# Attention inside a PE-bound network: scores of two heads issued in turn in the two row halves, softmaxes interleaved, near biases loaded when the job opens

## The chip, the cores and the metric

The kernel runs on one core of a Trainium2 chip. The core has a matmul engine (TensorE, PE in the profile; its weight loads are listed as PEld), a vector engine (VectorE, DVE), an activation engine (ScalarE, ACT), a general engine (GpSimd, POOL) and an engine that issues the DMA transfers (SyncE, SP). Each works through its own instruction list in order, and they wait for each other through semaphores. The metric is device time in microseconds, as the median of several runs.

## The reference, cut to what matters

Two layers of a transformer-like network work on 256 context and 256 latent tokens of 1024 channels. Each layer is a gated feed-forward half, a token mixer with four branches, and a second feed-forward half. Two branches of the mixer are attention with four heads of 64 channels, and latent queries see the local latent keys and all context keys:

```python
def neighbourhood_attention(q, k, v, kc, vc, rel_bias):
...
    s_loc = jnp.einsum('brnqhd,brnkchd->brnhqkc', qg, kg).astype(jnp.float32) * scale + bias
    s_loc = jnp.where(col_valid[None, None, :, None, :, None, :], s_loc, NEG_INF)
    s_ctx = jnp.einsum('brnqhd,blhd->brnhql', qg, kc).astype(jnp.float32) * scale
...
    probs = jax.nn.softmax(scores, axis=-1).astype(v.dtype)
```

The window branch does the same with a mask in place of the bias and with one more score, a learned sink per head, in the softmax. Context queries see the 256 context keys alone; they are needed only in the first layer, because the output is the latent stream.

## The kernel before, in words

All activations lie channels on partitions, tokens along the free side. The large products are made to fp32 accuracy from two fp32r parts: every weight tile is loaded by SP (line 128, three buffers `w`), split by ACT (`wh`, line 150) and DVE (`wl`, line 151), and each product of 128 channels is three PE instructions (`mm3`, lines 191 to 193). PE accumulates in eight banks: `A` has three, `B` two, `C`, `D` and `E` one each. One ordered list fixes the sequence of weight tiles.

Smaller work is placed beside the large products. A generator (`job`) does a piece and yields the nanoseconds of product time after which it wants to go on. `term` calls `spend(1.25 * columns)` after its three products (640 for 512 columns, 320 for 256), which advances a planning clock and lets at most one waiting piece run. `until(key)` runs waiting pieces at once until a job is done. This order is the program's; the build's scheduler then orders the instructions of each engine, and lets an instruction go ahead of earlier ones when those still wait for a buffer or an operand and it does not.

The mixer opens two attention jobs with the generator `attend`: "near" right after the keys, queries and values of the neighbourhood branch, and "window" later, within the gated merge. A unit is two heads and 128 queries. There are eight units per job in layer 0 (four context, four latent) and four in layer 1 (latent only). `attend` overlaps three units per round: `turn` transposes the weights of unit b through bank `C` (line 658) and ACT copies them out (line 660); `scores` multiplies keys and queries of unit a into a bank `B` and calls `softmax`; `values` multiplies the turned weights of unit c into bank `D` (line 689). An fp32 matmul of the program shows as two PE instructions in the profile. In `scores` (line 675) a head uses partitions 0 to 63 or 64 to 127, 256 keys at a time; latent units have two such halves of keys, context units one. In `values` the two heads already alternate, one into columns 0 to 63 of the array and one into 64 to 127.

`softmax` serves one head: bias and row maximum on DVE (lines 636 to 644), Exp with its sum on ACT (line 646), reciprocal and scaling on DVE (lines 650 and 651).

`na_bias` loads the bias of two heads with eight small DMAs into two tiles of tag `a` (line 567) and adds the mask into two tiles of tag `nb` (line 571). It is called from `scores`, when the first head of a pair has issued its products. Tag `a` has four buffers and also serves the softmax weights and their transposes. Tag `nb` has two and also serves a running sum of the norms.

Of the kernel before, what the change touches and what calls it, by code (L numbers as in the profile page):

```python
# [10 lines left out]
AF = mybir.ActivationFunctionType  # L11
ALU = mybir.AluOpType
# [10 lines left out]
NEG = -1e30  # L23
# [12 lines left out]
class Net:  # L36
# [15 lines left out]

    BUFS = dict(b=12, nb=2, ya=4, yp=4, m=8, a=4, l=5, r=3, t=2)
    BANKS = dict(A=3, B=2, C=1, D=1, E=1)
# [12 lines left out]

# [1 line left out]
    def plan(self):  # L69
# [85 lines left out]
    def apart(self, k):  # L155
        """Weights kept beside the ring: the last ones of a phase, whose two segments lie far apart."""
        return k[0] == "wo" and k[2] == 3 or k[0] == "dn" and k[3:] == (1, 7)
# [7 lines left out]

# [1 line left out]
    def later(self, ns, fn):  # L167
# [19 lines left out]

# [1 line left out]
    def mm3(self, ps, wh, wl, xh, xl, first, last):  # L189
# [110 lines left out]

# [1 line left out]
    def norm(self, l, i, rng):  # L302
# [93 lines left out]
    def first_tiles(self, W, P, H):  # L396
        """The first hidden tiles, as far as the modulation of their operands has come."""
        def terms(m, j):
            for k in (2 * j, 2 * j + 1):
                for g in range(2):  # L400
                    self.term(P[m][g], W[m], 1024 * g, H, *ALL, k)

        self.first_step(0)
        for j in range(4):
            terms(0, j)
            if j < 3:
                self.first_step(j + 1)
            terms(1, j)

    def finish_stream(self, parts, last, add, nxt):  # L410
        """Last output chunks by segment, each segment's norm beside the products that follow."""
        for r in parts:
            for c in last:
                add(c, r)
                for s in self.segs(r):
                    if nxt:
                        self.norm_square(nxt, c, s)
# [84 lines left out]

# [1 line left out]
    def softplus_terms(self, l):  # L504
# [52 lines left out]
    def na_bias(self, l, pr):  # L557
        nc = self.nc
        src = self.a["nb"]
        nb = []  # L560
        for h in (2 * pr, 2 * pr + 1):
            raw = self.blk("a", (128, 2, 4, 64))
            for qb in range(2):
                for r in range(2):
                    o = src.offset + (l * 4 + h) * 465 + (7 - (2 * qb + r)) * 31 - 48
                    ap = bass.AP(tensor=src.tensor, offset=o, ap=[[1, 64], [31, 4], [1, 64]])
                    nc.sync.dma_start(raw[64 * r:64 * r + 64, qb], ap)  # L567
            t = self.blk("nb", (128, 2, 4, 64))
            mask = self.cst[:, C_NM:C_NM + 256].rearrange("p (a b) -> p a b", b=64)
            for qb in range(2):  # L570
                nc.vector.tensor_tensor(t[:, qb], raw[:, qb, :, ::-1], mask, op=ALU.add)
            nb.append(t[:].rearrange("p q a b -> p q (a b)"))
        return nb
# [57 lines left out]

    def softmax(self, S, nk, bias, sink):
        nc = self.nc
        m = self.small((128, 4), "mx", 6)
        if bias is not None:
            nc.vector.tensor_tensor_reduce(out=S[:, 256:512], in0=S[:, 256:512], in1=bias, scale=1.0, scalar=NEG,
                                           op0=ALU.add, op1=ALU.max, accum_out=m[:, 0:1])
            nc.vector.tensor_reduce(m[:, 1:2], S[:, 0:256], axis=AX, op=ALU.max)
            nc.vector.tensor_tensor(m[:, 0:1], m[:, 0:1], m[:, 1:2], op=ALU.max)
        else:  # L640
            nc.vector.tensor_reduce(m[:, 0:1], S[:, 0:nk], axis=AX, op=ALU.max)
        if sink is not None:
            nc.vector.tensor_tensor(m[:, 0:1], m[:, 0:1], sink, op=ALU.max)
        nc.vector.tensor_scalar(m[:, 0:1], m[:, 0:1], -1.0, None, op0=ALU.mult)
        p = self.blk("a")
        nc.scalar.activation(p[:, :nk], S[:, :nk], AF.Exp, bias=m[:, 0:1], accum_out=m[:, 1:2])
        if sink is not None:
            nc.scalar.activation(m[:, 2:3], sink, AF.Exp, bias=m[:, 0:1])
            nc.vector.tensor_tensor(m[:, 1:2], m[:, 1:2], m[:, 2:3], op=ALU.add)
        nc.vector.reciprocal(m[:, 3:4], m[:, 1:2])  # L650
        nc.vector.tensor_scalar(p[:, :nk], p[:, :nk], m[:, 3:4], None, op0=ALU.mult)
        return p

# [9 lines left out]
    def attend(self, step, segs, out, keys, queries, value, biases, sink):  # L663
        """One unit is two heads and 128 queries; scores, turned weights and values of three units overlap."""
        nc = self.nc
# [3 lines left out]

        def scores(u, hh):  # L670
            pr, sg, qb = u
            rows, qw = slice(64 * hh, 64 * hh + 64), slice(128 * qb, 128 * qb + 128)
            S = self.ps("B")
            for j in range(nk(u) // 256):
                nc.tensor.matmul(S[:, 256 * j:256 * j + 256], queries(sg, j)[rows, pr, qw], keys(j, pr)[rows],  # L675
                                 start=True, stop=True)
            if pr not in bias:
                bias[pr] = biases(pr)
            P[u, hh] = self.softmax(S, nk(u), bias[pr](hh, qb) if sg else None, sink(pr, hh))

        def values(u):
# [9 lines left out]
            if qb == 1:  # L691
                if len(out) == pr:
                    out.append(self.blk("ya"))
                nc.scalar.activation(out[pr][:, 256 * sg:256 * sg + 256], y, AF.Copy)

        while self.pending:
            yield 300
        for i in range(len(U) + 2):
            a, b, c = (U[i - d] if 0 <= i - d < len(U) else None for d in range(3))
            if b:  # L700
                T[b, 0] = self.turn(P.pop((b, 0)), nk(b))
                yield step
            if a:
                scores(a, 0)
                yield step
            if c:
                values(c)
                yield step
            if b:
                T[b, 1] = self.turn(P.pop((b, 1)), nk(b))  # L710
                yield step
            if a:
                scores(a, 1)
            yield 2 * step
# [43 lines left out]
    def mixer(self, l, H, nxt):  # L758
# [19 lines left out]

        # the first products take the operands chunk by chunk, as the norm delivers them
        two = lambda: self.blk("b", (128, 2, 256))  # L780
# [37 lines left out]

        # short convolution
        view = lambda q: q[:, lo:hi].rearrange("p (s t) -> p s t", s=ns)  # L820
# [43 lines left out]

        # gated merge
        M, MP = [None] * KC, [None] * KC
# [170 lines left out]
```

## Time and profile before

| what | value |
|---|---|
| median of 3 runs | 2096.6 us (2094.93 to 2097.59) |
| span of the profiled execution | 2092.9 us |
| median less that span | 3.7 us |
| PE, PEld | 2065.0, 1755.2 us busy |
| DVE, ACT, POOL | 1325.4, 808.5, 86.1 us busy |
| mean granted clock of PE | 0.995 of 2.4 GHz |
| attention, layer 0: near, window | about 464 to 568, 637 to 730 us |
| attention, layer 1: near, window | about 1663 to 1725, 1772 to 1826 us |

The span runs from the first to the last instruction of one profiled execution; what lies around it is in the runs' times alone. A matmul's busy time holds its fill and drain, which overlap with its neighbours, so start times of consecutive matmuls tell more of cost than durations do. "Idle before" is the time an engine stood still in front of an instruction, with what ended it behind the arrow.

### The profile page before, as it was taken

The numbers are of one execution on the slowest core, as the hardware profiler recorded it, in microseconds if no ns is written. First come the engines' busy times: TensorE is split into PE (matmuls) and PEld (weight loads), VectorE is DVE, ScalarE is ACT, GpSimd is POOL, SyncE is SP. The second block draws the span as 40 slices with busy tenths as digits, with TensorE's granted clock in tenths as the row PEclk, the third lists the DMA queues.
The fourth block names the chain that finished last, engine by engine and source line by source line (L and its number), as shares of the span: only waits on it lengthen the run. The fifth ranks groups of instructions, "written<-read, shape, count | busy, mean of one in ns | idle before, by whom it ended". The sixth has DMA issues, their size and how long they took to land.

```text
span 2092.9 us, 29695 instructions
## 1 busy us (share of the span) xinstructions
PE 2065.0 (99%) x11937; PEld 1755.2 (84%) x11937; DVE 1325.4 (63%) x2393; ACT 808.5 (39%) x1321; POOL 86.1 (4%) x90
## 2 busy tenths in 40 slices
PE   7999999999999999999999999999999999999999
PEld 4888888896797788888888888788888989999999
DVE  4887887476546545677533367778844768775554
ACT  3322222365434434332222233222223656564443
POOL 0000000110010000100000010000001101000000
PEclk9999999999999999999999999999999999999999
DMA  9454555412122124145432234445543234363453
GB/s 331 181 182 173 202 199 164 137 69 52 63 91 76 63 100 145 70 161 182 154 116 88 75 130 161 162 170 201 194 117 133 74 87 141 128 226 143 171 196 118
DMA packets 61403, 294.46 MB, mean 141 GB/s; under 512 B 14672, under 2 KB 16336, under 8 KB 38224
## 3 DMA queue, kind: packets, MB, share of 16 engines
q1 hardware_dynamic: 61264, 292.55, 39.9%
q8 instruction: 94, 1.54, 0.3%
q14 instruction: 45, 0.37, 0.1%
HBM read 291.48 MB, written 1.05 MB: 140 GB/s over the span
## 4 chain that ended last, share of the span: by engine, by line
PE 94%; DMA 2%; issue 2%; SPq 0%; DVE 0%; POOL 0%; ACT 0%; POOLq 0%; DVEq 0%; ACTq 0%
PE A L191 19%; PE A L192 18%; PE A L193 18%; PE B L191 11%; PE B L193 11%; PE B L192 11%; PE B L675 2%; PE D L689 1%; DMA b<-in_mod 1%; PE D L265 1%; PE C L658 1%; DMA a<-in_nb 1%; PE E L728 1%; SPq L567 0%; PE E L601 0%
## 5 line engine op out<-in xcount | busy, mean ns | idle before, releaser
L150 ACT ACTIVATE wh<-w 128x1024 fp32r<-128x1024 f32 (+2 forms) x476 | 430.4, 906 | 870.9 <-PE A L192 403.9
L151 DVE TENSOR_TENSOR wl<-w,wh 128x1024 fp32r<-128x1024 f32 (+2 forms) x476 | 490.3, 1031 | 316.6 <-ACT wh L150 311.8
L191 PE MATMUL A<-h,wh 128*128 128x512 f32 (+1 forms) x1440 | 511.4, 355 | 6.2 <-ACT wh L150 3.8
L193 PE MATMUL A<-h,wl 128*128 128x512 f32 (+1 forms) x1440 | 497.6, 346 | 0.0
L192 PE MATMUL A<-h,wh 128*128 128x512 f32 (+1 forms) x1440 | 497.0, 345 | 0.0
L191 PEld LDWEIGHTS A<-h,wh 128*128 128x128 f32 x1440 | 273.8, 190 | 64.7 <-issue 18.6
L256 DVE SCALAR_TENSOR_TENSOR ya<-w,sc,ya 128x512 f32<-128x512 f32 x448 | 310.2, 747 | 13.3 <-DMA w<-in_mod 12.1
L193 PEld LDWEIGHTS A<-h,wl 128*128 128x128 f32 x1440 | 273.8, 190 | 34.2 <-DVE wl L151 1.7
L192 PEld LDWEIGHTS A<-h,wh 128*128 128x128 f32 x1440 | 274.0, 190 | 30.3 <-issue 1.1
L191 PE MATMUL B<-h,wh 128*128 128x512 f32 (+1 forms) x736 | 262.0, 356 | 0.0
L192 PE MATMUL B<-h,wh 128*128 128x512 f32 (+1 forms) x736 | 261.7, 356 | 0.0
L193 PE MATMUL B<-h,wl 128*128 128x512 f32 (+1 forms) x736 | 261.6, 355 | 0.0
L191 PEld LDWEIGHTS B<-h,wh 128*128 128x128 f32 x736 | 140.0, 190 | 19.9 <-ACT wh L150 0.4
L192 PEld LDWEIGHTS B<-h,wh 128*128 128x128 f32 x736 | 139.7, 190 | 19.6 <-issue 0.4
L193 PEld LDWEIGHTS B<-h,wl 128*128 128x128 f32 x736 | 139.7, 190 | 19.4
L455 DVE TENSOR_TENSOR t<-t,B 128x512 f32<-128x512 f32 (+1 forms) x88 | 54.2, 619 | 118.7 <-PE B L193 117.6
L330 POOL TENSOR_TENSOR nb<-nb,l 128x256 f32<-128x256 f32 x45 | 45.9, 1037 | 1351.9 <-ACT l L328 1351.9
L191 PE MATMUL A<-b,wh 128*128 128x512 f32 (+1 forms) x246 | 85.1, 346 | 0.0
L193 PE MATMUL A<-b,wl 128*128 128x512 f32 (+1 forms) x246 | 85.0, 345 | 0.0
L192 PE MATMUL A<-b,wh 128*128 128x512 f32 (+1 forms) x246 | 84.9, 345 | 0.0
L191 PE MATMUL B<-b,wh 128*128 128x512 f32 (+1 forms) x204 | 73.5, 360 | 0.0
L192 PE MATMUL B<-b,wh 128*128 128x512 f32 (+1 forms) x204 | 73.4, 360 | 0.0
(271 smaller groups left out, 2996.1 us busy)
## 6 DMA issues: line engine op xcount, KB each, us to landing
w<-in_gu SPq DMA_DIRECT2D x88, 1024.0 KB, 4.8
w<-in_mod SPq DMA_DIRECT2D x64, 1024.0 KB, 4.8
w<-in_dn SPq DMA_DIRECT2D x64, 704.0 KB, 4.0
w<-in_gb SPq DMA_DIRECT2D x64, 640.0 KB, 3.9
w<-in_fm SPq DMA_DIRECT2D x10, 1024.0 KB, 4.8
w<-in_tm SPq DMA_DIRECT2D x10, 1024.0 KB, 4.9
w<-in_wo SPq DMA_DIRECT2D x8, 1024.0 KB, 4.8
b<-in_mod SPq DMA_DIRECT2D x20, 256.0 KB, 5.7
```

The lines of the kernel that those rows point to most:

```text
L150: nc.scalar.activation(hi[i][:, :e], t[:, o:o + e], AF.Copy)
L151: nc.vector.tensor_tensor(lo[i][:, :e], t[:, o:o + e], hi[i][:, :e].bitcast(F32), op=ALU.subtract)
L191: mm(ps, wh, xh, start=first, stop=False)
L192: mm(ps, wh, xl, start=False, stop=False)
L193: mm(ps, wl, xh, start=False, stop=last)
L256: nc.vector.scalar_tensor_tensor(acc, w[:, k], sv, acc, op0=ALU.mult, op1=ALU.add)
L265: nc.tensor.matmul(g[32 * q:32 * q + 32, :], self.sel[:, j], self.part[s - 1 + q // 2][q % 2], start=(r in (1, 5)), stop=last, tile_positi ...
L330: nc.gpsimd.tensor_tensor(n["acc"][s], n["acc"][s], sq, op=ALU.add)
L455: nc.vector.tensor_tensor(s[:, lo:hi], s[:, lo:hi], ps[1][:, lo:hi], op=ALU.mult)
L658: nc.tensor.transpose(pt[:, j], p[:, 128 * j:128 * j + 128], self.ident)
L675: nc.tensor.matmul(S[:, 256 * j:256 * j + 256], queries(sg, j)[rows, pr, qw], keys(j, pr)[rows], start=True, stop=True)
L689: nc.tensor.matmul(y[64 * hh:64 * hh + 64, 128 * qb:128 * qb + 128], value(j, pr, hh), T[u, hh][:, j], start=(j == 0), stop=(j == n - 1), ...
```

## The change

`scores` takes both heads of a unit at once. For each half of the keys it issues head 0's product (rows 0 to 63) and then head 1's (rows 64 to 127), each into its own bank `B`. `softmax` works on both heads: maximum, bias and Exp of head 0, then of head 1, then one addition of the sinks and one reciprocal for both, then the two scalings. In a round of `attend` the order becomes `values` of c, `turn` of b's head 0, `scores` of a, `turn` of b's head 1, with steps of 1, 1, 2 and 2 where there were five pieces with steps of 1, 1, 1, 1 and 2.

The biases of both head pairs are requested when the job opens, before it waits for its operands. Their raw tiles have a tag of their own, `nr`, with four buffers, `nb` has four instead of two, and `a` six instead of four. The scratch that the build sets aside in SBUF for DMAs shrinks to 1024 bytes a partition. Some comments go as well and are left out of the diff.

```diff
@@ -50,7 +50,7 @@
         self.n += 1
         return f"{s}{self.n}"
 
-    BUFS = dict(b=12, nb=2, ya=4, yp=4, m=8, a=4, l=5, r=3, t=2)
+    BUFS = dict(b=12, nb=4, nr=4, ya=4, yp=4, m=8, a=6, l=5, r=3, t=2)
     BANKS = dict(A=3, B=2, C=1, D=1, E=1)
 
     def blk(self, tag, shape=(128, 512), dt=F32):
...
@@ -559,7 +559,7 @@
         src = self.a["nb"]
         nb = []
         for h in (2 * pr, 2 * pr + 1):
-            raw = self.blk("a", (128, 2, 4, 64))
+            raw = self.blk("nr", (128, 2, 4, 64))
             for qb in range(2):
                 for r in range(2):
                     o = src.offset + (l * 4 + h) * 465 + (7 - (2 * qb + r)) * 31 - 48
...
@@ -630,26 +630,32 @@
         self.later(3000, scale)
 
     def softmax(self, S, nk, bias, sink):
-        nc = self.nc
-        m = self.small((128, 4), "mx", 6)
-        if bias is not None:
-            nc.vector.tensor_tensor_reduce(out=S[:, 256:512], in0=S[:, 256:512], in1=bias, scale=1.0, scalar=NEG,
-                                           op0=ALU.add, op1=ALU.max, accum_out=m[:, 0:1])
-            nc.vector.tensor_reduce(m[:, 1:2], S[:, 0:256], axis=AX, op=ALU.max)
-            nc.vector.tensor_tensor(m[:, 0:1], m[:, 0:1], m[:, 1:2], op=ALU.max)
-        else:
-            nc.vector.tensor_reduce(m[:, 0:1], S[:, 0:nk], axis=AX, op=ALU.max)
-        if sink is not None:
-            nc.vector.tensor_tensor(m[:, 0:1], m[:, 0:1], sink, op=ALU.max)
-        nc.vector.tensor_scalar(m[:, 0:1], m[:, 0:1], -1.0, None, op0=ALU.mult)
-        p = self.blk("a")
-        nc.scalar.activation(p[:, :nk], S[:, :nk], AF.Exp, bias=m[:, 0:1], accum_out=m[:, 1:2])
-        if sink is not None:
-            nc.scalar.activation(m[:, 2:3], sink, AF.Exp, bias=m[:, 0:1])
-            nc.vector.tensor_tensor(m[:, 1:2], m[:, 1:2], m[:, 2:3], op=ALU.add)
-        nc.vector.reciprocal(m[:, 3:4], m[:, 1:2])
-        nc.vector.tensor_scalar(p[:, :nk], p[:, :nk], m[:, 3:4], None, op0=ALU.mult)
-        return p
+        nc = self.nc
+        m = self.small((128, 2, 4), "mx", 6)
+        P = []
+        for hh in range(2):
+            v = m[:, hh]
+            if bias is not None:
+                nc.vector.tensor_tensor_reduce(out=S[hh][:, 256:512], in0=S[hh][:, 256:512], in1=bias(hh), scale=1.0,
+                                               scalar=NEG, op0=ALU.add, op1=ALU.max, accum_out=v[:, 0:1])
+                nc.vector.tensor_reduce(v[:, 1:2], S[hh][:, 0:256], axis=AX, op=ALU.max)
+                nc.vector.tensor_tensor(v[:, 0:1], v[:, 0:1], v[:, 1:2], op=ALU.max)
+            else:
+                nc.vector.tensor_reduce(v[:, 0:1], S[hh][:, 0:nk], axis=AX, op=ALU.max)
+            if sink(hh) is not None:
+                nc.vector.tensor_tensor(v[:, 0:1], v[:, 0:1], sink(hh), op=ALU.max)
+            nc.vector.tensor_scalar(v[:, 0:1], v[:, 0:1], -1.0, None, op0=ALU.mult)
+            P.append(self.blk("a"))
+            nc.scalar.activation(P[hh][:, :nk], S[hh][:, :nk], AF.Exp, bias=v[:, 0:1], accum_out=v[:, 1:2])
+            if sink(hh) is not None:
+                nc.scalar.activation(v[:, 2:3], sink(hh), AF.Exp, bias=v[:, 0:1])
+        if sink(0) is not None:
+            nc.vector.tensor_tensor(m[:, :, 1:2], m[:, :, 1:2], m[:, :, 2:3], op=ALU.add)
+        nc.vector.reciprocal(m[:, :, 3:4], m[:, :, 1:2])
+        for hh in range(2):
+            nc.vector.tensor_scalar(P[hh][:, :nk], P[hh][:, :nk], m[:, hh, 3:4], None, op0=ALU.mult)
+        return P
 
     def turn(self, p, nk):
         nc = self.nc
...
@@ -661,22 +667,23 @@
         return pT
 
     def attend(self, step, segs, out, keys, queries, value, biases, sink):
         nc = self.nc
         U = [(pr, sg, qb) for pr in range(2) for sg in segs for qb in range(2)]
         P, T, Y, bias = {}, {}, {}, {}
         nk = lambda u: 512 if u[1] else 256
 
-        def scores(u, hh):
+        def scores(u):
             pr, sg, qb = u
-            rows, qw = slice(64 * hh, 64 * hh + 64), slice(128 * qb, 128 * qb + 128)
-            S = self.ps("B")
+            qw = slice(128 * qb, 128 * qb + 128)
+            S = [self.ps("B"), self.ps("B")]
             for j in range(nk(u) // 256):
-                nc.tensor.matmul(S[:, 256 * j:256 * j + 256], queries(sg, j)[rows, pr, qw], keys(j, pr)[rows],
-                                 start=True, stop=True)
-            if pr not in bias:
-                bias[pr] = biases(pr)
-            P[u, hh] = self.softmax(S, nk(u), bias[pr](hh, qb) if sg else None, sink(pr, hh))
+                for hh in range(2):
+                    rows = slice(64 * hh, 64 * hh + 64)
+                    nc.tensor.matmul(S[hh][:, 256 * j:256 * j + 256], queries(sg, j)[rows, pr, qw], keys(j, pr)[rows],
+                                     start=True, stop=True)
+            P[u] = self.softmax(S, nk(u), (lambda hh: bias[pr](hh, qb)) if sg else None, lambda hh: sink(pr, hh))
 
         def values(u):
             pr, sg, qb = u
...
@@ -693,24 +700,23 @@
                     out.append(self.blk("ya"))
                 nc.scalar.activation(out[pr][:, 256 * sg:256 * sg + 256], y, AF.Copy)
 
+        for pr in range(2):
+            bias[pr] = biases(pr)
         while self.pending:
             yield 300
         for i in range(len(U) + 2):
             a, b, c = (U[i - d] if 0 <= i - d < len(U) else None for d in range(3))
-            if b:
-                T[b, 0] = self.turn(P.pop((b, 0)), nk(b))
-                yield step
-            if a:
-                scores(a, 0)
-                yield step
             if c:
                 values(c)
                 yield step
             if b:
-                T[b, 1] = self.turn(P.pop((b, 1)), nk(b))
+                T[b, 0] = self.turn(P[b][0], nk(b))
                 yield step
             if a:
-                scores(a, 1)
+                scores(a)
+                yield 2 * step
+            if b:
+                T[b, 1] = self.turn(P.pop(b)[1], nk(b))
             yield 2 * step
 
     def recurrence(self, segs, out, U, bd, sp2, hb, step):
...
@@ -1023,7 +1029,7 @@
     from concourse.bass_utils import run_bass_kernel_spmd
 
     A = layout(**{k: np.asarray(v) for k, v in inputs.items()})
-    nc = bacc.Bacc("TRN2", target_bir_lowering=False, num_devices=1)
+    nc = bacc.Bacc("TRN2", target_bir_lowering=False, num_devices=1, dynamic_dma_scratch_size=1024)
     arrays, a = {}, {}
     for k, v in A.items():
         arrays[f"in_{k}"] = v
```

## Rows read from the trace of the kernel before

**Rows 1.** Spans and granted clock; the page's busy time by engine.

```profile
core 0: 2092.9 us, clock 0.995
...
PE 2065.0 (99%) x11937; PEld 1755.2 (84%) x11937; DVE 1325.4 (63%) x2393; ACT 808.5 (39%) x1321; POOL 86.1 (4%) x90
```

**Rows 2.** The page's chain that ended last, by line.

```profile
PE A L191 19%; PE A L192 18%; PE A L193 18%; PE B L191 11%; PE B L193 11%; PE B L192 11%; PE B L675 2%; PE D L689 1%; DMA b<-in_mod 1%; PE D L265 1%; PE C L658 1%; DMA a<-in_nb 1%; PE E L728 1%; SPq L567 0%; PE E L601 0%
```

**Rows 3.** Windows, first near attention: length, busy PE, PEld, DVE, ACT, POOL, clock, DMA.

```profile
464.00:568.00 104.00, 100.87 (x495) 73.18 (x494) 65.28 (x158) 54.77 (x99) 0.00 (x0) 0.98 0.21 55
```

**Rows 4.** Waits of PE: total us, times, longest us.

```profile
PE C L658 <- DVE a L651: 4.6, 2, 3.1
...
PE B L675 <- ACT a L646: 1.5, 1, 1.5
```

**Rows 5.** Timeline of PE around a latent and a context score call: start, us.

```profile
478.90 0.40 PE L192 MATMUL A<-h,wh 128*128 128x512 f32 x1
479.13 0.40 PE L193 MATMUL A<-h,wl 128*128 128x512 f32 x1
479.46 1.13 PE L675 MATMUL B<-b,b 64*128 64x256 f32 x4
...
480.85 0.40 PE L192 MATMUL A<-h,wh 128*128 128x512 f32 x1
...
513.99 0.40 PE L193 MATMUL A<-h,wl 128*128 128x512 f32 x1
514.31 0.70 PE L675 MATMUL B<-b,b 64*128 64x256 f32 x2
...
515.27 0.39 PE L192 MATMUL A<-h,wh 128*128 128x512 f32 x1
```

**Rows 6.** Lines by form, ACT's Exp: count, busy us, mean ns, idle before.

```profile
L646 ACT ACTIVATE a<-B,mx 128x512 f32<-128x512 f32 x32 | 21.9, 685 | 25.4 <-DVE mx L644 20.8 <-PE D L689 4.4
...
L646 ACT ACTIVATE a<-B,mx 128x256 f32<-128x256 f32 x16 | 7.6, 472 | 14.7 <-DVE mx L644 10.5 <-PE D L689 3.9 <-PE C L658 0.2
```

**Rows 7.** Timeline of the value products in layer 1's near attention.

```profile
1686.12 1.09 PE L689 MATMUL D<-a,b 128*64 128x128 f32 x16
...
1697.29 0.43 PE L689 MATMUL D<-a,b 128*64 128x128 f32 x2
```

**Rows 8.** Timeline of the bias loads of head pair 1, layer 0.

```profile
510.99 6.63 SPq L567 DMA_DIRECT2D a<-in_nb  x8
...
517.66 0.42 DVE L571 TENSOR_TENSOR nb<-a,cst 128x256 f32<-128x256 f32 x1 [3.46 <-DMA a<-in_nb]
...
521.31 0.41 PE L658 MATMUL C<-cst,a 128*128 128x128 f32 x2 [3.13 <-DVE a L651]
```

**Rows 9.** Windows behind the two stalls (columns as in rows 3).

```profile
523.30:526.80 3.50, 3.50 (x21) 2.54 (x19) 3.50 (x10) 0.38 (x1) 0.00 (x0) 0.51 0.51 180
1700.90:1707.80 6.90, 5.43 (x29) 4.09 (x28) 4.36 (x18) 2.86 (x7) 0.00 (x0) 0.51 0.10 42
```

**Rows 10.** Timeline of SP early in the run.

```profile
40.21 0.33 SPq L767 DMA_DIRECT2D bd<-in_bd  x1
58.87 0.33 SPq L128 DMA_DIRECT2D w<-in_mod  x1
```

**Rows 11.** Lines by form, softmax and transposes (columns as in rows 6).

```profile
L660 ACT ACTIVATE a<-C 128x512 f32<-128x512 f32 x32 | 18.9, 592 | 10.8 <-PE C L658 7.7 <-DVE nb L571 3.1
L651 DVE TENSOR_SCALAR a<-a,mx 128x512 f32<-128x512 f32 x32 | 15.5, 484 | 1.3
L638 DVE TENSOR_REDUCE mx<-B 128x1 f32<-128x256 f32 x32 | 13.5, 422 | 0.7
...
L646 ACT ACTIVATION_READ_ACCUMULATOR a<-B,mx 128x1 f32 x48 | 9.3, 194 | 0.0
L650 DVE RECIPROCAL mx<-mx 128x1 f32<-128x1 f32 x48 | 7.7, 160 | 7.1 <-ACT a L646 6.5
...
L646 ACT ACT_TABLE_LOAD x5 | 6.4, 1283 | 0.1
```

## Prediction

> **What bounds the kernel now.** I read the busy shares first: the matmul engine PE is busy 99% of the span [rows 1]. Busy matmul time alone does not prove a bound, so next came the chain of work that ended last: the large products of lines 191 to 193 hold 88% of the span, the score products of line 675 hold 2% and the loads of `in_nb` 1% [rows 2]. Everything PE does is on the path; whatever PE no longer has to do, or no longer waits for, comes off the end one for one as long as the other engines keep up. In the stretch of the first near attention the vector engine DVE is busy 65.3 of 104 us and the scalar engine ACT 54.8 [rows 3], so there is room to run some 10% faster there. The third view is PE's own waits: within the attention jobs they are two waits for `a` of line 651 (the scaled softmax, 4.6 us) and one for `a` of line 646 (1.5 us) [rows 4]. The rest of the 28 us without PE work (2092.9 - 2065.0) stands elsewhere, and the change does not touch it.
>
> **Scores side by side.** A head's score product contracts over 64 channels and so uses half the rows of the array. It runs between full products, and what it costs is what it pushes them apart. Latent queries (two key halves, four PE instructions, as an fp32 product is two): from the product in front at 479.13 to the second one behind at 480.85 are 1.72 us; undisturbed products stand 0.23 apart, so 1.72 - 0.46 = 1.26 us. Context queries (two instructions): 515.27 - 513.99 - 0.46 = 0.82 us [rows 5]. The Exp counts give the calls: 32 with 512 keys, 16 with 256 [rows 6]. All scores: 32 x 1.26 + 16 x 0.82 = 53.4 us of PE's path. Inside a call, two more instructions add 1.13 - 0.70 = 0.43 us, so 0.215 each; of the 1.26 us, 0.86 is streaming and 0.40 is the cost of getting in and out of the half-array shape (0.82 - 0.43 = 0.39 says the same).
>
> The change issues both heads' products in turn, one into rows 0 to 63 and one into rows 64 to 127, each into a bank of its own. No row of before shows two row halves at once, so I bound it. Nothing at all, if the second bank is not free in time and the pair falls apart into two calls as now; a loss I exclude, as no instruction is added. If the pair stays together but runs one after the other, 24 entries and exits are saved, 24 x 0.40 = 9.5 us. Best: they run together, a pair costs what one call does now, and half of 53.4 goes: 26.7 us. The nearest row is line 689, where the two heads' value products lie in two column halves and are written in turn. One head's first two instructions alone took 0.43 us; all 16 took 1.09 [rows 7]. So the other 14 took 0.66; at 0.108 each (half of 0.215, half the columns) they would take 1.51 in series, and 0.65 if two always run in lockstep. That is lockstep to within the reading. I take the best end, 26.7 us.
>
> One rule speaks against that. The Trainium skill, TensorE: Matmul & The Clock Gate, section "Part 3: Packing small matmuls — row/col tiling", says that matmuls start and end strictly in program order; with two instructions per fp32 product, the second of head 0 then keeps head 1 back by one place. By that rule a pair has one place more, 0.215 us x 24 = 5.2 us, and the sum would be 21.5 instead of 26.7. The trace disagrees for column halves, where the reading was 0.65 predicted by lockstep against 0.66 taken.
>
> **Bias loads.** The second stall belongs to the near bias. Today the biases of head pair 1 are loaded only when its first scores are issued: eight loads leave SP from 510.99 in 6.63 us, DVE's bias addition at 517.66 stood 3.46 us waiting for the load, and with DVE in order the softmax scaling behind it came late, so that PE idled 3.13 us at line 658 [rows 8]. In the second layer the same thing costs the other two waits, 1.47 + 1.54 us [rows 4]. After these idle times the granted clock is 0.51, its lower level of 1.2 GHz, for 3.5 and 6.9 us, with PE busy 3.50 and 5.43 us of them [rows 9]; work at half clock loses half its time: 1.75 + 2.7 us. The stall is worth 3.13 + 1.47 + 1.54 + 1.75 + 2.7 = 10.6 us.
>
> After, all 16 loads of a layer are issued when the job opens, into four tiles of their own (`nr`) and not into the shared ring `a`, and there are four `nb` tiles instead of two, so pair 1 no longer waits for pair 0. The build lets a load out as soon as its buffer is free: `bd`, asked for by the mixer, left at 40.21 [rows 10]. So I expect layer 0's loads far ahead of the 464 us where the attention begins, and layer 1's once layer 0's additions are done. What it costs: SP time and traffic. Sixteen loads at 6.63 / 8 = 0.83 us are 13.3 us of SP; if they go out behind `bd` they fit before the next weight load at 58.87, 18.7 us later [rows 10]. Without that cover they push a weight load back by 13.3 us in each layer, so the bounds are 0 and 26.6 us; I take 1 us, since among PE's waits in the attention jobs none is for a weight [rows 4]. The eight bias additions per layer stay eight and sit in DVE's slack [rows 3]. The bounds of the gain are 0 (the DVE wait just moves to another place) and 10.6; I take 10.6, because the loads lose the two buffer waits that made them late. What could be late next is the softmax itself.
>
> **Interleaved softmaxes and the new order.** Per pair of heads one reciprocal is saved and, with a sink, one addition: 24 x 0.16 = 3.8 us of DVE [rows 11], off the path, worth 0. But head 0's weights now wait for head 1's Exp. With reductions of 0.42 (two per head), some three small operations of 0.16, Exp 0.685 plus 0.194 for its sum and scaling 0.484 [rows 6, 11], the chain from scores to scaled weights is about 1.3 + 0.88 + 0.16 + 0.48 = 2.8 us today and 2.6 + 0.88 + 0.16 + 0.48 = 4.1 after. From the scores to `turn` of head 0 the new order leaves two double steps and a single one: in layer 0, 870 and 1740 ns of planned time round up to 2 and 3 groups of three products (3 x 0.23 = 0.69 us, the plan's 640 ns), so 8 x 0.69 = 5.5 us plus the value products. That holds 4.1 with 1.4 to spare; worth 0.
>
> Tighter: `values` now comes first in the round, a double step behind `turn` of head 1: 3 x 0.69 = 2.1 us where it was 9 x 0.69 = 6.2. The transposes (4 x 0.108) and the copy out (0.592) need 1.0 us [rows 11], so 1.1 is left for ACT's queue. Bounds: 0, and the last rival below. I take 0: the rows show DVE and ACT a third or more idle there [rows 3], and two more `a` buffers take away the wait for a free one. The smaller DMA scratch only makes room for the new tiles.
>
> **Sum.** 26.7 + 10.6 - 1 = 36.3 us off the profiled 2092.9 gives a span of 2056.6. The median of the runs, 2096.6, lies 3.7 above the span, so 2060 us, 1.7% faster. This kernel's runs agree to 0.13%, so 0.2% is about what a measurement can tell from no change.
>
> **Rivals.**
> Row halves do not overlap: 9.5 instead of 26.7, and 2060 becomes 2077. For it: no row shows row halves at once. Against: column halves run in lockstep. Chance 14%.
> The pair overlaps, but head 1's first pass waits for head 0's second: one place more per pair, 24 x 0.215 = 5.2 us, 2065. Against: the 14 instructions of [rows 7] would then need seven places of 0.108, 0.76 us, and took 0.66. The skill's rule above is this case. Chance 8%.
> The bias stall moves instead of going: DVE waits for an early load, or a weight load is late behind 16 bias loads. 5 to 12 us back: 2065 to 2072. For it: the stalled addition came 6.7 us after the first issue [rows 8], and each layer now sends twice as many loads at once. Against: four own buffers. Chance 12%.
> The other side: `values` waits for `turn`. If ACT has a table load (1.283) and both heads' Exps with their sums (0.88 each) ahead of the copy, that is 3.0 us against 1.1 of slack, 1.9 late per unit; 24 units make 46 us, and 2060 becomes 2106. It decides from 36.3 / 24 = 1.5 us late per unit on. Against: the tables change five times in the whole run at line 646 [rows 11], so it cannot strike each unit. Chance 4%.
> My forecast, 2055 to 2064: 62%.
>
> Range: 2054 (the forecast's low end, with a little for a stall I did not see) to 2078, which takes in the strict order, the moved stall and the serial case and leaves out about 1 in 10; the serial case sets the upper end. Faster 0.94, same 0.02, slower 0.04.
>
> **What would show it.** Line 675: 160 matmuls still, but in 24 groups; 8 instructions of a latent pair in about 1.15 us if they overlap, 2.0 if not. Waits of PE at lines 658 and 675 gone, the clock at its upper level through both near attentions, the `in_nb` loads of layer 0 far ahead of 464 us. No new wait of PE at line 689 for the `a` that ACT copies out. Wrong would be: pairs of 2.0 us, or PE idle over 1 us per unit in front of the values.

## The result, and the profile after

The changed kernel takes 2064.15 us (median of 4, 2062.49 to 2066.55), before beside it 2095.76: a ratio of 0.9848, 95% interval 0.9836 to 0.9860. That is 31.6 us faster, where 36.6 were forecast (2060). The profiled executions differ by less, 2092.9 - 2064.8 = 28.1 us, because that of before was one of its quicker ones and that of after its slowest of four.

The page of after, answering to [rows 1] and [rows 2]: span, busy times, the chain by line.

```profile
core 0: 2064.8 us, clock 0.995
...
PE 2037.9 (99%) x11937; PEld 1740.5 (84%) x11937; DVE 1311.4 (64%) x2357; ACT 805.3 (39%) x1321; POOL 87.8 (4%) x90
...
PE A L191 19%; PE A L192 18%; PE A L193 18%; PE B L191 11%; PE B L192 11%; PE B L193 11%; PE B L684 1%; DMA b<-in_mod 1%; PE D L696 1%; DMA w<-in_gu 1%; PE C L664 1%; PE D L265 1%; DVE ya L256 1%; PE E L734 1%; DVE wl L151 0%
```

PE executes as many instructions as before in 27 us less. The score products (now line 684) fell from 2% of the chain to 1%, and the `in_nb` loads, 1% before, are gone from it. A load of `in_gu`, a weight, has come in with 1%.

The timeline of PE around a latent score pair, columns as in [rows 5].

```profile
488.13 0.39 PE L192 MATMUL A<-h,wh 128*128 128x512 f32 x1
488.35 0.39 PE L193 MATMUL A<-h,wl 128*128 128x512 f32 x1
488.67 1.13 PE L684 MATMUL B<-b,b 64*128 64x256 f32 x8
489.74 0.50 PE L191 MATMUL A<-h,wh 128*128 128x512 f32 x1
490.07 0.40 PE L192 MATMUL A<-h,wh 128*128 128x512 f32 x1
```

Eight instructions take the 1.13 us that four took. From the product in front to the second one behind are 490.07 - 488.35 = 1.72 us, as before for one head; less 0.46, a pair costs 1.26 us. That is lockstep in full: the two heads run side by side. Taken the same way over all score calls, they cost the path 53.6 us before and 26.9 us after.

The windows of after that answer to [rows 3] and the first of [rows 9], and PE's waits, columns as in [rows 4].

```profile
464.00:568.00 104.00, 104.00 (x580) 80.95 (x581) 66.92 (x154) 58.92 (x107) 0.64 (x1) 1.00 0.19 64
523.30:526.80 3.50, 3.50 (x17) 2.86 (x18) 3.50 (x9) 2.67 (x6) 0.00 (x0) 1.00 0.49 154
```

```profile
PE D L315 <- ACT l L313: 5.8, 2, 5.6
PE C L272 <- ACT t L269: 4.4, 1, 4.4
...
PE C L664 <- DVE a L657: 0.7, 1, 0.7
```

In the stretch of the first near attention PE now never stands and the granted clock stays at 1.00. The three attention waits of before are all gone. The 0.7 us at line 664 (the transposes, waiting for the scaled softmax) are a new wait, at 1755.61 us in layer 1's window attention, where PE had none before. The first row of the waits belongs to the start of every execution. The second row is new too: PE stands 4.4 us at line 272, in the modulation, far from the attention.

To place the time I cut both traces where the norms broadcast their factors (line 360, bank E), work that the change does not touch. Before, the four marks around the two mixers:

```profile
416.95 0.71 PE L360 MATMUL E<-cst,r 128*128 128x128 f32 x4 [0.35 <-POOL r L356]
877.16 0.71 PE L360 MATMUL E<-cst,r 128*128 128x128 f32 x4 [0.36 <-POOL r L356]
...
1624.58 0.71 PE L360 MATMUL E<-cst,r 128*128 128x128 f32 x4 [0.35 <-POOL r L356]
1894.90 0.71 PE L360 MATMUL E<-cst,r 128*128 128x128 f32 x4 [1.04 <-POOL r L356]
```

After:

```profile
425.70 0.71 PE L360 MATMUL E<-cst,r 128*128 128x128 f32 x4 [0.35 <-POOL r L356]
864.32 0.71 PE L360 MATMUL E<-cst,r 128*128 128x128 f32 x4 [0.36 <-POOL r L356]
...
1611.73 0.71 PE L360 MATMUL E<-cst,r 128*128 128x128 f32 x4 [0.35 <-POOL r L356]
1867.40 0.71 PE L360 MATMUL E<-cst,r 128*128 128x128 f32 x4 [1.03 <-POOL r L356]
```

| stretch | before | after | gain |
|---|---|---|---|
| start to first mark | 416.95 | 425.70 | -8.75 |
| layer 0's mixer | 460.21 | 438.62 | 21.59 |
| between the mixers | 747.42 | 747.41 | 0.01 |
| layer 1's mixer | 270.33 | 255.67 | 14.66 |
| rest of the span | 198.0 | 197.4 | 0.6 |

The two mixers give 36.25 us. For them alone the forecast had 26.7 + 10.6 = 37.3; its 36.3 holds 1 us off for the loads. The start, where next to nothing was to be lost, takes 8.75 back.

**What happens in the start.** SP's timeline of after, from where [rows 10] ended:

```profile
60.80 0.33 SPq L128 DMA_DIRECT2D w<-in_mod  x1
61.17 1.36 SPq L567 DMA_DIRECT2D nr<-in_nb  x2
...
66.64 0.59 SPq L567 DMA_DIRECT2D nr<-in_nb  x1
...
83.22 3.24 SPq L567 DMA_DIRECT2D nr<-in_nb  x5
...
104.23 2.58 SPq L567 DMA_DIRECT2D nr<-in_nb  x4
```

All 16 loads of layer 0 leave between 61 and 107 us, in between the weight loads. The view of the DMAs in the stretch from 60 to 108 us: first the packets, then each load's count, size and median us from issue to landing. Before:

```profile
DMA packets 1429, 10.47 MB, mean 218 GB/s; under 512 B 153, under 2 KB 153, under 8 KB 153
...
w<-in_gu SPq DMA_DIRECT2D x5, 1024.0 KB, 4.8
w<-in_mod SPq DMA_DIRECT2D x4, 1024.0 KB, 5.4
```

After:

```profile
DMA packets 4553, 10.26 MB, mean 214 GB/s; under 512 B 3399, under 2 KB 3399, under 8 KB 3399
...
w<-in_mod SPq DMA_DIRECT2D x5, 1024.0 KB, 5.1
w<-in_gu SPq DMA_DIRECT2D x4, 1024.0 KB, 9.4
nr<-in_nb SPq DMA_DIRECT2D x16, 64.0 KB, 8.8
```

The bytes moved are nearly the same, but in three times as many packets, and an `in_gu` weight of 1 MB lands in 9.4 us instead of 4.8. The median of `in_mod`, 5.1, hides two late ones: those that left at 70.23 and 91.09 us, behind bias loads, took 9.2 and 12.1. Who stands for it shows in ACT's and PE's timelines of after, and in the windows behind (columns as in [rows 3]):

```profile
106.11 1.06 ACT L150 ACTIVATE wh<-w 128x1024 fp32r<-128x1024 f32 x1 [4.17 <-DMA w<-in_gu]
...
109.59 0.58 ACT L269 ACTIVATE t<-D 128x512 f32<-128x512 f32 x1
```

```profile
110.22 1.12 PE L272 MATMUL C<-cst,t 128*128 128x128 f32 x4 [4.36 <-ACT t L269]
```

```profile
60.00:108.10 48.10, 45.86 (x205) 36.71 (x204) 37.54 (x56) 14.58 (x20) 0.00 (x0) 1.00 0.74 213
108.10:115.00 6.90, 4.78 (x14) 3.92 (x15) 6.28 (x13) 1.61 (x3) 0.00 (x0) 0.51 0.64 34
```

ACT splits the weight late, and the copy that PE wants is queued behind the splits. PE stands 4.36 us, and then the granted clock is 0.51, the 1.2 GHz level, up to 115 us. The same two windows of before:

```profile
60.00:108.10 48.10, 48.10 (x219) 38.89 (x218) 41.99 (x67) 16.06 (x21) 0.00 (x0) 1.00 0.59 218
108.10:115.00 6.90, 6.90 (x32) 5.73 (x31) 6.90 (x11) 2.60 (x3) 0.00 (x0) 1.00 0.39 152
```

There 32 matmuls more are done: 7.4 us at the 0.23 us between products. How far PE falls back shows at the products of line 265 just ahead of the wait, first of before, then of after:

```profile
101.49 1.07 PE L265 MATMUL D<-ya,sel 128*32 128x512 f32 x8
103.44 1.07 PE L265 MATMUL D<-ya,sel 128*32 128x512 f32 x8
```

Here after is 1.95 us late, at the first mark 8.75, so 6.8 us are lost behind line 265. The 1.95 were lost earlier, with the granted clock at 0.57 from 36 to 40 us. There it was 0.57 to 0.70 in the executions of e1, e3, e6, e7, e9 and e10 too, and 1.00 in those of before, e2, e4, e5, e8, e11 and e12. Loads that leave early and loads that are held stand in both groups, so these 1.95 us are no effect of the early loads.

### The profile page after: what moved, and what is told of

Read it like the earlier page. It is cut to its first block, busy times and chain, and to the rows that moved or that the text cites. A ratio compares the mean times of both kernels' runs of the same rounds, so it can differ in the third digit from the quotient of the medians.

```text
span 2064.8 us, 29629 instructions
## 1 busy us (share of the span) xinstructions
PE 2037.9 (99%) x11937; PEld 1740.5 (84%) x11937; DVE 1311.4 (64%) x2357; ACT 805.3 (39%) x1321; POOL 87.8 (4%) x90
## 4 chain that ended last, share of the span: by engine, by line
PE 94%; DMA 2%; DVE 2%; ACT 1%; issue 1%; POOL 0%; SPq 0%; POOLq 0%; ACTq 0%; DVEq 0%
PE A L191 19%; PE A L192 18%; PE A L193 18%; PE B L191 11%; PE B L192 11%; PE B L193 11%; PE B L684 1%; DMA b<-in_mod 1%; PE D L696 1%; DMA w<-in_gu 1%; PE C L664 1%; PE D L265 1%; DVE ya L256 1%; PE E L734 1%; DVE wl L151 0%
## 5 line engine op out<-in xcount | busy, mean ns | idle before, releaser
L256 DVE SCALAR_TENSOR_TENSOR ya<-w,sc,ya 128x512 f32<-128x512 f32 x448 | 309.5, 745 | 10.9 <-DMA w<-in_mod 9.9
L192 PEld LDWEIGHTS A<-h,wh 128*128 128x128 f32 x1440 | 274.1, 190 | 30.9 <-issue 0.6
```

Source lines behind the costliest of these rows:

```text
L192: mm(ps, wh, xl, start=False, stop=False)
L256: nc.vector.scalar_tensor_tensor(acc, w[:, k], sv, acc, op0=ALU.mult, op1=ALU.add)
```

## The experiments

In this table a gain is the median of before in the same session less that of the kernel, us. The ratio has its 95% interval.

| kernel | median | ratio | gain |
|---|---|---|---|
| after | 2064.15 | 0.9848 [0.9836, 0.9860] | 31.6 |
| e1, all, loads held to 355 us | 2062.70 | 0.9839 [0.9826, 0.9852] | 34.4 |
| e2, scores and softmax alone | 2075.92 | 0.9895 [0.9881, 0.9908] | 21.2 |
| e3, bias part alone | 2088.95 | 0.9958 [0.9945, 0.9972] | 8.1 |
| e4, bias part alone, held | 2089.39 | 0.9960 [0.9948, 0.9973] | 7.7 |
| e5, e1, heads one after the other | 2063.13 | 0.9843 [0.9828, 0.9857] | 32.7 |
| e6, e1, softmax by head | 2061.70 | 0.9839 [0.9822, 0.9855] | 34.4 |
| e7, e1, old round | 2062.03 | 0.9838 [0.9823, 0.9853] | 33.8 |
| e8, one head pair's biases | 2062.66 | 0.9833 [0.9817, 0.9849] | 33.2 |
| e9, held to 416 us | 2070.08 | 0.9875 [0.9860, 0.9890] | 25.8 |
| e10, two raw tiles | 2059.25 | 0.9830 [0.9815, 0.9844] | 36.9 |
| e11, loads spread out | 2075.13 | 0.9902 [0.9888, 0.9917] | 21.0 |
| e12, two raw tiles, four `a` | 2058.99 | 0.9822 [0.9805, 0.9838] | 37.8 |

**The two parts, and the early loads (e1 to e4).** My theory: the early loads cost the start some 7 us, and holding them back returns it. The rival: the start differs from one execution to the next by itself. e1 is after with a write that each raw tile must wait for:

```diff
             raw = self.blk("nr", (128, 2, 4, 64))
+            nc.gpsimd.tensor_tensor(raw[:, :, 0, 0], self.x[0][:, 0:2], self.x[0][:, 0:2], op=ALU.add)
```

> The changed kernel with one addition: a two-column GpSimd write of each raw bias tile that reads the stream x first, so that a layer's bias loads cannot leave before about 353 us (layer 0) and 1540 us (layer 1). My theory: the changed kernel gave back 6.8 us in the start, where early bias loads slow the weight loads (PE idle 4.4 us before line 272 at 110 us, then 4.78 us of PE work at the lower clock, 2.4 us). Holding the loads gives 2064.2 - 6.8 = 2057 us and no PE wait of more than 1 us between 40 and 400 us. Rival 1: that gap is not due to the bias loads; then 2064 us and the gap stays. Rival 2: the loads collide with weight loads where they now leave; then a new PE wait near 360 us and over 2060 us.

e2 is after without the bias part:

```diff
-    BUFS = dict(b=12, nb=4, nr=4, ya=4, yp=4, m=8, a=6, l=5, r=3, t=2)
+    BUFS = dict(b=12, nb=2, ya=4, yp=4, m=8, a=4, l=5, r=3, t=2)
...
-            raw = self.blk("nr", (128, 2, 4, 64))
+            raw = self.blk("a", (128, 2, 4, 64))
...
+            if pr not in bias:
+                bias[pr] = biases(pr)
...
-        for pr in range(2):
-            bias[pr] = biases(pr)
```

> Scores in pairs, softmaxes interleaved, new round order, but biases loaded as before (at the pair's first scores, into tag a with 4 buffers, nb with 2). My theory: row halves overlap and are worth 26.7 us, both stalls of head pair 1 stay: 2095.8 - 26.7 = 2069 us, with PE waits of 3 us (layer 0) and about 3 us (layer 1) for the softmax and the lower clock behind them. Rival: the pairs are worth only what the total of 31.6 leaves after 10.6 for the biases, 21.0: 2075 us.

e3 is before with the bias part alone, and e4 is e3 with e1's write.

```diff
-            raw = self.blk("a", (128, 2, 4, 64))
+            raw = self.blk("nr", (128, 2, 4, 64))
...
-            if pr not in bias:
-                bias[pr] = biases(pr)
...
+        for pr in range(2):
+            bias[pr] = biases(pr)
```

> The kernel before with the bias part alone: all biases requested when the job opens, tags nr 4, nb 4, a 6, small DMA scratch; scores and softmax head by head as before. My theory: 10.6 us gained at the attention, 6.8 lost in the start: 2092 us, with PE idle about 4 us near 110 us. Rival 1: the start stall needs the other part too: 2085 us. Rival 2: the stall at head pair 1 is filled by another wait: 2095.8 to 2103 us.

> As the run with the bias part alone, but each layer's loads held back until x is there (353 and 1540 us). My theory: the stall at head pair 1 alone, 10.6 us: 2085 us. Rival: another wait takes its place: 2093 to 2096 us.

The same marks in e3:

```profile
425.27 0.71 PE L360 MATMUL E<-cst,r 128*128 128x128 f32 x4 [0.35 <-POOL r L356]
880.63 0.71 PE L360 MATMUL E<-cst,r 128*128 128x128 f32 x4 [0.35 <-POOL r L356]
...
1628.07 0.71 PE L360 MATMUL E<-cst,r 128*128 128x128 f32 x4 [0.35 <-POOL r L356]
1892.38 0.71 PE L360 MATMUL E<-cst,r 128*128 128x128 f32 x4 [1.04 <-POOL r L356]
```

By them e3's mixers last 455.36 and 264.31 us: 4.85 + 6.02 = 10.9 us gained. From e3 to after they lose another 16.74 + 8.64 = 25.4, which is what the pairs are worth once the stall is gone. e2's last 445.89 and 262.01, 14.3 + 8.3 = 22.6 us gained, so there the stall still costs 36.25 - 22.6 = 13.7, more than the 10.9 that e3 gained. Why it costs more was not tested. In e2's timelines, first DVE, then PE:

```profile
511.26 0.42 DVE L571 TENSOR_TENSOR nb<-a,cst 128x256 f32<-128x256 f32 x1 [3.34 <-DMA a<-in_nb]
515.43 0.43 DVE L571 TENSOR_TENSOR nb<-a,cst 128x256 f32<-128x256 f32 x1 [2.35 <-DMA a<-in_nb]
```

```profile
516.54 1.34 PE L698 MATMUL D<-a,b 128*64 128x128 f32 x10 [5.37 <-ACT a L666]
```

PE stands 5.37 us there, against 3.13 in [rows 8], and now in front of the value products. In layer 0 the eight loads left from 498.73 us on, and the last bias addition came 16.7 us later; before, it came 13.0 us later. The forecast of 2069 for e2 was missed (2075.92), and the rival's 2075 came closer. The profiled execution, 2071.39, is the quickest of four; what the other three (2075.8 to 2076.8) lost is not seen.

The start: with 16 early loads (e3) PE fell 6.5 us behind between 82 and 117 us, where after fell 6.8; without them (e1, e2, e4) 0. So the early loads are the cause, and not chance. But the hold has a price: e1 and e4 send the loads from 355 us on, beside other weight loads, and lose 2.7 and 3.5 us at 367 to 374 us, with a new PE wait of 1.6 us at line 272. That is e1's second rival, and why its 2057 and e4's 2085 were missed. By the stretches a hold from 61 to 355 us is worth 6.8 - 2.7 = 4.1 us (after to e1) and 6.5 - 3.5 = 3.0 (e3 to e4). The gains of the table differ by 2.8 and -0.4, which their intervals, some 2.5 us to either side, cannot tell from that or from nothing.

**Do the row halves keep to program order?** (e5)

```diff
-            for j in range(nk(u) // 256):
-                for hh in range(2):
-                    rows = slice(64 * hh, 64 * hh + 64)
+            for hh in range(2):
+                rows = slice(64 * hh, 64 * hh + 64)
+                for j in range(nk(u) // 256):
```

> The version with held bias loads (2062.7 us measured), but in a pair of scores all products of head 0 are issued before those of head 1, where they alternated. It changes only latent units (16 of the 24), which have two products a head. Theory A, each row half has its own queue, and the engine looks at least four instructions ahead: no change, 2063 us, eight instructions of a pair in about 1.15 us. Theory B, it looks only to the next product: head 1 starts with head 0's last instruction, seven places of 0.215 instead of four: 16 x 3 x 0.215 = 10 us more, 2073. Theory C, strictly in order across heads: 16 x 0.86 = 14 us more, 2077.

e5's timeline of PE:

```profile
482.13 1.14 PE L685 MATMUL B<-b,b 64*128 64x256 f32 x8
```

All four instructions of head 0 now come ahead of the first of head 1, and the eight still take 1.14 us. In strict order head 1 could start only with head 0's last instruction: three places of 0.215 more, 1.78 us. Against e1 the time differs by less than either's interval. The strict order has fallen.

**The softmax and the round (e6, e7).** e6 scales each head on its own:

```diff
-        if sink(0) is not None:
-            nc.vector.tensor_tensor(m[:, :, 1:2], m[:, :, 1:2], m[:, :, 2:3], op=ALU.add)
-        nc.vector.reciprocal(m[:, :, 3:4], m[:, :, 1:2])
-        for hh in range(2):
-            nc.vector.tensor_scalar(P[hh][:, :nk], P[hh][:, :nk], m[:, hh, 3:4], None, op0=ALU.mult)
+                nc.vector.tensor_tensor(v[:, 1:2], v[:, 1:2], v[:, 2:3], op=ALU.add)
+            nc.vector.reciprocal(v[:, 3:4], v[:, 1:2])
+            nc.vector.tensor_scalar(P[hh][:, :nk], P[hh][:, :nk], v[:, 3:4], None, op0=ALU.mult)
```

> The version with held bias loads (2062.7 us), scores in pairs, but each head's softmax finished by itself (own addition of the sink, own reciprocal, scaling before the other head's reductions). My theory: the interleaving is off the path; 2062.7 within 2 us, and at most the one PE wait of 0.9 us for the scaled softmax at 1751 us goes. Rival: joining the two heads' small operations is part of the gain; then 2066 or more.

e7 moves `values(c)` back to the middle of the round:

```diff
-            if c:
-                values(c)
-                yield step
...
+            if c:
+                values(c)
+                yield step
             if b:
                 T[b, 1] = self.turn(P.pop(b)[1], nk(b))
```

> The version with held bias loads, but with the round in the old order: turn of head 0, scores of both heads, values, turn of head 1. My theory: the new place of the values costs nothing, so 2063 us and within 2 of it. Rival: the short way from turn to values costs PE time that shows nowhere as a wait but in the order of the products; then this is faster, below 2060.

Gains of 34.4 and 33.8 against e1's 34.4: nothing that the medians can tell. In e6 the one PE wait of 0.7 to 0.9 us for the scaling goes, and layer 1's mixer lasts 255.03 us against e1's 255.90, so the interleaving cost about that.

**How many loads, and when (e8 to e12).** e8 leaves half of the loads out:

```diff
-            nb = self.na_bias(l, pr)
+            if pr == 0:
+                self.nb0 = self.na_bias(l, pr)
+            nb = self.nb0
```

> The changed kernel with the biases of head pair 0 used for pair 1 too (the biases of heads 2 and 3 are left out), so 8 bias loads a layer instead of 16, still early. If the loss in the start comes from the traffic of the bias loads beside the weight loads, the 6.7 us that PE falls behind between 80 and 150 us become 3 or less, and the run 2061. If it comes from having any of them in the queue at that place, 6 to 7 us stay and the run is 2064.

It did not test what it was meant to. Its loads, by line 567: count, ns, first and last start.

```profile
L567 SPq DMA_DIRECT2D nr<-in_nb x16: 597/615/1435, 59.3 to 104.4; - x16
```

Layer 1's eight loads took the two raw tiles that were free, so 16 loads stood in the start again, and the lag there was 7.1 us: the same number of loads, another purpose, the same loss.

Three other ways, each an edit of after: e10 limits the number by the tiles, e9 holds all loads on a part of the stream that is written later, and e11 holds each head's on another part. The edits, in that order:

```diff
-    BUFS = dict(b=12, nb=4, nr=4, ya=4, yp=4, m=8, a=6, l=5, r=3, t=2)
+    BUFS = dict(b=12, nb=4, nr=2, ya=4, yp=4, m=8, a=6, l=5, r=3, t=2)
```

```diff
+            nc.gpsimd.tensor_tensor(raw[:, :, 0, 0], self.x[7][:, 256:258], self.x[7][:, 256:258], op=ALU.add)
```

```diff
+            nc.gpsimd.tensor_tensor(raw[:, :, 0, 0], self.x[2 * h][:, 0:2], self.x[2 * h][:, 0:2], op=ALU.add)
```

> The version with held bias loads, but held on the last block of x instead of the first, so they leave at about 407 to 420 us, behind the feed-forward half, and not at 353 among its weight loads. By my stretches the two mixers gain 21.6 + 14.6 = 36.2 us, and nothing is given back in the start or at 373 us: 2097 - 36 = 2061 us or a little less. Rival: with 40 us to go the additions of the bias are late, DVE waits for a load and PE shows a wait of over 1 us between 420 and 500 us: 2063 or more.

> The changed kernel with two raw bias tiles instead of four: nothing is left out, but only 8 loads can leave in the start, the other 24 from 353 us on. (The run with half the loads per layer still sent 16 in the start, since layer 1's took the free tiles, so it did not test the amount.) If the 6.7 us that PE falls behind between 80 and 150 us come from the amount of traffic, they become 0 to 3: 2058 to 2061 us. If any load in the queue there costs them, 6 to 7 stay: 2064.

> Loads held as in the version with held bias loads, but head h waits for block 2h of x, so they leave four at a time between 353 and 410 us and not in one burst at 353. My theory: no loss in the start, none at 370 us (the held version lost 2 us there), both mixers keep their gain of 36 us: 2060 us against 2097. Rival: the last head's loads land late, DVE stands at its bias addition and a wait appears near 445 us, as in the version held on the last block: 2064 or more.

e10, the loads from 60 to 108 us, and the two windows of the start:

```profile
w<-in_mod SPq DMA_DIRECT2D x5, 1024.0 KB, 6.0
w<-in_gu SPq DMA_DIRECT2D x5, 1024.0 KB, 5.0
nr<-in_nb SPq DMA_DIRECT2D x8, 64.0 KB, 6.3
```

```profile
60.00:108.10 48.10, 48.10 (x218) 38.92 (x217) 42.04 (x65) 16.79 (x22) 0.00 (x0) 1.00 0.68 214
108.10:115.00 6.90, 6.90 (x33) 5.69 (x32) 6.90 (x11) 1.55 (x2) 0.00 (x0) 1.00 0.59 215
```

With eight early loads the `in_gu` weights land in 5.0 us (those of `in_mod` in 6.0), PE never stands from 60 to 115 us, and no wait at line 272 takes its place; the mixers are as short as after's (438.53 and 255.30 us). The median, 2059.25, is where e10's forecast had it if the amount counts.

e9 and e11 are the other side. A wait of PE in e9's timeline, and two of DVE in e11's, ahead of the second mixer:

```profile
447.81 1.65 PE L735 MATMUL E<-b,bd 128*128 128x256 f32 x3 [3.76 <-DVE b L545]
```

```profile
1589.04 0.42 DVE L572 TENSOR_TENSOR nb<-nr,cst 128x256 f32<-128x256 f32 x1 [2.36 <-DMA nr<-in_nb]
1593.76 0.43 DVE L572 TENSOR_TENSOR nb<-nr,cst 128x256 f32<-128x256 f32 x1 [4.29 <-DMA nr<-in_nb]
```

The additions stand in DVE's queue where the job opens. A load that is not there by then holds up everything behind: in e9 the convolution of line 545, for which PE stood 6.3 us in two waits, in e11 the norms ahead of both mixers (PE at line 341 waited 2.2 and 0.8 us ahead of the first, 4.9 ahead of the second). Both rivals came true, at 2070.08 and 2075.13 us; e11 also lost 2.4 us near 370 us, where its forecast had none. Held loads can come too late as well as too early.

e12 also goes back to four `a`:

```diff
-    BUFS = dict(b=12, nb=4, nr=4, ya=4, yp=4, m=8, a=6, l=5, r=3, t=2)
+    BUFS = dict(b=12, nb=4, nr=2, ya=4, yp=4, m=8, a=4, l=5, r=3, t=2)
```

> The version with two raw bias tiles (2059.25 us), with tag a back to its four buffers. In the new order at most five tiles of a are wanted at once, and a turned tile is allocated only when its source has been read. My theory: the two more buffers are worth nothing, 2059 us within 2. Rival, as the prediction had it: they take away a wait of ACT for a free tile that the new order would pass on to the values; then PE waits appear in front of the value products and the run is over 2063 us.

2058.99 us, not distinguishable from e10, so the two extra `a` are worth nothing here. It is the shortest of all: 37.8 us ahead of before. Its interval and after's, from different sessions, meet by a hair; that it beats after is shown by the start, where its first mark stands at 416.71 against 425.70 (2.2 of these 9.0 us are from ahead of 60 us, 6.8 from behind), with mixers of 438.57 and 255.73. Its span is 36.5 us below before's, where the forecast's sum was 36.3.

## Why the prediction came out as it did

**Scores side by side: right, mechanism and size.** 26.7 us were taken from the column halves of [rows 7]. Measured are 26.7 on the score calls (53.6 - 26.9) and 25.4 by the stretches; the 1.3 between them are not traced. Of its bounds, nothing and the serial 9.5 are excluded.

**The rule against it did not hold here.** The Trainium skill, TensorE: Matmul & The Clock Gate, section "Part 3: Packing small matmuls — row/col tiling", says that matmuls start and end strictly in program order. By the prediction's reading of that the pairs would cost 5.2 us more in all, and a latent pair would take 1.13 + 0.215 = 1.345 us, where it took 1.13. e5 shows the contrary more sharply: in its order head 1's first instruction lies four behind head 0's first, and both heads were done in the time of one.

**Bias stall: right.** 10.6 us were added up from waits and half-clock time; the mixers of e3 gained 10.9, by layers 4.85 and 6.02 against 4.88 and 5.7. It is not additive with the pairs: in e2 the remaining stall costs 13.7.

**The cost of the moved loads: the term that was mis-sized.** "I take 1 us, since among PE's waits in the attention jobs none is for a weight." It measured 6.8 us, within its bounds of 0 to 26.6. Two things failed in the step. The loads were expected behind `bd`, in the 18.7 us ahead of the weight load of 58.87. But a free buffer is not all that a load needs: the `nr` tiles had no earlier user, and yet the loads left 20 us behind `bd` (40.57), from 61.17 us on, between weight loads in SP's queue. And the cover was looked for in the attention jobs, while it had to be judged in the stretch where the loads would leave: there (60 to 116 us) ACT already waited 15.7 us for weights before; after it waited 30.9, in e10 19.8. The rival "a weight load is late behind 16 bias loads" had the mechanism and the size (5 to 12 us). It came true beside the forecast, not instead of it, which is why the time, 2064, lies between the forecast's 2055 to 2064 and the rival's 2065 to 2072.

**Softmax, round, `a`: 0, right to within 1 us.** The medians of e6, e7 and e12 show no difference. "With 1.4 to spare" did not hold everywhere: once, in layer 1's window attention, the scaled softmax came 0.7 us late. PE has no wait at line 696, so the last rival, 46 us for late values, did not occur.

**The sum.** Mixers 36.25 (pairs 25.4, stall 10.9) against 26.7 + 10.6 = 37.3; less 8.75 in the start, of which 1.95 is that execution's own, plus 0.6: 28.1 by the spans. That the mixers equal the forecast's 36.3 is chance, since it holds 1 us for the loads. With two raw tiles in place of four (e10, e12) the kernel comes to 2059, next to the forecast time, but that is another kernel than the one forecast.

**Open.** The 16 loads delay the weights by their packets, by SP's issue time (some 10 us over 45), or by both; landing, counted from the issue, doubled, so SP alone is not it, but the shares were not taken apart. Between 8 loads at no loss and 16 at 6.5 to 7.1 us no number was tried.

## What to carry to other kernels

Contractions over 64 channels cost half here when the products of two heads are issued next to each other in the two row halves, in turn or one head after the other. A load that is asked for early and has a free buffer can leave long before its use (here some 300 us ahead of the bias addition), so its cost is to be judged in the stretch where it will then leave, and the number of its buffers is a handle on that: two raw tiles instead of four gave the shortest times here. A load held to a later point can come too late (e9, e11), since its consumer stands in an in-order queue and stops what is behind it.

## What was not expected of the hardware

Row halves do not only overlap in turn: with four instructions for one half issued ahead of the first for the other, eight took 1.14 us, as in turn (1.13).

64 KB loads in packets of under 512 bytes cost far more than their bytes: with 16 of them, 1 MB in all, beside the weight loads the `in_gu` loads of 1 MB landed in 9.4 us instead of 4.8, at nearly equal total bytes (10.26 against 10.47 MB); with 8 they landed in 5.0.
